# Fifteen load buffers, later modulation pieces, and block heads by halves of their banks, in a hybrid diffusion layer on one core

## The chip, the cores and the metric

The kernel runs on one core of one Trainium2 chip. The metric is device time in microseconds (us) of one execution. A profiled execution of the same program gives the span and the records of each engine: TensorE (PE, with its weight loads PEld), VectorE (DVE), ScalarE (ACT), GpSimd (POOL) and SyncE (SP), which issues most of the loads.

## The reference

One layer of a hybrid backbone is applied to 128 context tokens and 128 latent tokens, with shared weights. All arithmetic is float32.

```python
def block(x, mod, p, lb, s0_hg, s0_gdn, rows):
    shift1, scale1, gate1, shift2, scale2, gate2 = jnp.split(mod, 6, axis=-1)
    h = rmsnorm(x, p['norm1_g']) * (1.0 + scale1) + shift1
    (hq, hi, hgo, hff, hfb, cu, cv, gqkv, ggo, ga, gbeta, gates) = jnp.split(
        h @ p['w_in'], np.cumsum(IN_SIZES)[:-1].tolist(), axis=-1)
    o_a, s_hg = hgrn2_branch(hq, hi, hgo, hff, hfb, lb, p['hg_onorm_g'], s0_hg)
    o_b = chunk_mlp_branch(cu, cv, p['cm_vnorm_g'], p['cm_ws'], p['cm_bs'])
    o_c, s_gdn = gdn_branch(gqkv, ggo, ga, gbeta, ...)
    g_a, g_b, g_c = jnp.split(jax.nn.sigmoid(gates), 3, axis=-1)
    merged = (g_a * (o_a @ p['w_br_hg']) + g_b * (o_b @ p['w_br_cm']) + g_c * (o_c @ p['w_br_gdn']))
    x = x + gate1 * (merged @ p['w_out'])
    h2 = rmsnorm(x, p['norm2_g']) * (1.0 + scale2) + shift2
    x = x + gate2 * (jnp.square(jax.nn.relu(h2 @ p['w_ff1'])) @ p['w_ff2'])
    return x, s_hg, s_gdn
```

`mod` is `silu(c) @ w_mod + b_mod`, once with the context vector and once with the latent one. The model width is 2048, the hidden width of the channel sub-layer 8192. A final RMSNorm follows, and the final states of two branches are returned.

## The kernel before

All weights stream once through the chip, in units of 128 x 1024 floats (512 KB), and the 256 tokens stand still. A weight unit is loaded into a raw buffer by SP, then split into a rounded high part (`wh`, a cast on ACT) and a low part (`wl`, a subtraction on DVE); each product is three matmuls, high by high, low by high and high by low. The pair of split parts has its own buffers: three pairs, and two more during the opening (slots 8 and 9).

The program is written out by a planner in Python. `Clock` and `Meter` keep a planned time for each engine and buffer. `run_stream` walks through a list of steps. `issue()` emits loads as long as a raw buffer is in the list `raws`; `front()` emits the split of units ahead of their use, as long as a pair is in the list `pairs`; then the matmuls of the step are emitted. Between matmul groups `pump()` emits pieces of other work ("fillers": generators that run until they must wait), as long as ACT and DVE are planned less than a margin (1.8 us, 3.0 in the opening) ahead of TensorE. What is emitted later stands later in its engine's queue. Modulation pieces are the background filler and come last.

The opening (`start_steps`) has 88 units: 64 modulation units (`wmods`, for shift1 and scale1), which are used whole and unsplit, eight for each eighth of the width, and between them 16 units of the FF columns of `w_in` and 8 of the first half of FB. `lend` is 88. The raw buffers are three of their own (pool `rawp`, tag `raw`, used in turn) and, in the opening, five slots (3 to 7) of the large buffers, of which a load takes half. A slot goes back to the list only while fewer than `lend - 8` loads are issued; from then on the three own buffers are all there is. Modulation units give their buffer back when they are multiplied, the others when they are split.

The rest of the modulation (chunks 2 to 5) is 128 pieces done on DVE (`mods`): each is a load `mraw` of 512 KB and two multiply-and-sum passes (`junk<-mraw,cb`). The first two are loaded when the generator is created, at the 49th modulation unit; piece m is begun only when `quota(m)` units have been multiplied. `marks` are unit counts: a = 88, b before the last branch, and c, d, e about the end of the first sub-layer.

A block is one product with 1024 columns: 16 units (8 for the branch projections) into four PSUM banks of 512, out of six (`psb`), so that two banks of the next block are free while the last one is evacuated. In orientation B a bank takes two groups of 256 tokens, in A one group of 512 columns. A unit is one k-tile and runs through all four banks in order; `evac` empties them at the end, on ACT or DVE. For a branch (`branch`) evacuation is a multiplication of each bank by its gate on DVE, with `tail` as a filler behind it for the second and third branch. Most operations are recorded on line 173, that of the planner's wrapper, so tiles tell them apart: `raw` are loads, `pb` the block banks, `pf` the fillers' banks, `z` the large slots.

Of the kernel before, what the change touches and what calls it, by code (L numbers as in the profile page):

```python
# [7 lines left out]
F32 = mybir.dt.float32  # L8
F32R = mybir.dt.float32r
U8 = mybir.dt.uint8  # L10
AF = mybir.ActivationFunctionType
ALU = mybir.AluOpType
# [184 lines left out]
class Backbone:  # L197
# [194 lines left out]
    def run_stream(self, steps):  # L392


        nc = self.nc
        units = [s["unit"] for s in steps if "unit" in s]
        raw, hl = [], {}
        st = dict(dma=0, front=0)
        t = self.t

        raws = [None] * 3 + [3, 4, 5, 6, 7]
        pairs = [None] * 3 + [8, 9]

        def issue():
            while raws and st["dma"] < len(units):
                n = st["dma"]
                z = raws.pop(0)
                u = units[n]
                if z is None:
                    w = self.rawp.tile([P, NB], F32, tag="raw", name=self.nm("raw"))[:, :u.shape[1]]  # L410
                else:
                    w = self.slot(z, [P, NB])
                nc.sync.dma_start(w, u)
                raw.append((w, self.clock.dma + DMA1, z))
                st["dma"] += 1

        def front():
            n = st["front"]
            s = steps[n]
            st["front"] += 1  # L420
            if "unit" not in s:
                return
            w, at, z = raw.pop(0)
            if "whole" in s:
                hl[n] = (w, None, z, at)
                return
            c = w.shape[1]
            p = None if "own" in s else pairs.pop(0)
            if "own" in s:
                hi, lo = s["own"]()  # L430
            elif p is None:
                hi = self.hlp.tile([P, NB], F32R, tag="wh", name=self.nm("wh"))[:, :c]
                lo = self.hlp.tile([P, NB], F32R, tag="wl", name=self.nm("wl"))[:, :c]
            else:
                both = self.slot(p, [P, 2, NB], F32R)
                hi, lo = both[:, 0, :], both[:, 1, :]
            self.split(hi, lo, w)
            hl[n] = (hi, lo, p, max(t["act"], t["dve"]) + READY)
            if z is None or st["dma"] < self.lend - 8:
                raws.append(z)  # L440
            issue()

        issue()
        for i, s in enumerate(steps):
            while st["front"] < len(steps) and (pairs or not {"whole", "own"}.isdisjoint(steps[st["front"]])) and not ("hold" in s and st["front"] > i):
                if st["front"] > i and (raw and raw[0][1] > t["pe"] + 1.5 or len(hl) > 4) or not raw and "unit" in steps[st["front"]]:
                    break
                front()
            if s["kind"] == "mm":
                hi, lo, p, _ = hl.pop(i)  # L450
                s["do"](hi, lo)
                self.units += 1
                if "whole" in s:
                    if p is None or st["dma"] < self.lend - 8:
                        raws.append(p)
                    issue()
                    self.pump()
                    continue
                self.next = min((v[3] for v in hl.values()), default=0.0)
                self.pump()  # L460
                self.next = 0.0
                if "own" not in s and (p is None or st["dma"] < self.lend):
                    pairs.append(p)
            elif s["kind"] == "call":
                s["do"]()

    def block(self, units, nk, xh, xl, evac, orient="B", pre=None, late=False):


        nc = self.nc  # L470
        st = {}
        steps = []
        per = nk // len(units)
        cols = NB // per
        nb = max(4 // per, 1)

        def do(u, hi, lo):
            if u == 0:
                if pre is not None:
                    pre()  # L480
                st["b"] = [self.psb.tile([P, 512], F32, tag="b", name=self.nm("pb")) for _ in range(nb)]
            if u >= len(units) - 2:
                self.evac = self.t["pe"] + 24 * 0.12 * (len(units) - u)
            for k in range(u * per, u * per + per):
                off = (k - u * per) * cols
                ah, al = xh(k), xl(k)
                for c in range(8 if late else 0):
                    o = st["b"][c // 2][:, (c % 2) * 256:(c % 2) * 256 + 256]
                    for m, w in enumerate((hi, lo)):
                        nc.tensor.matmul(o, lhsT=w[:, c * P:c * P + P], rhs=ah, start=(k == 0 and m == 0 and c % 2 == 0),  # L490
                                         stop=False, skip_group_check=True)
                for c in range(2 * cols // min(cols, 512) if orient == "A" else 2 * nb):
                    if orient == "B":
                        o = st["b"][c // 2][:, (c % 2) * 256:(c % 2) * 256 + 256]
                        w = slice(off + c * P, off + c * P + P)
                        ops = ((hi[:, w], ah), (lo[:, w], ah), (hi[:, w], al))
                        first, lastc = c % 2 == 0, c % 2 == 1
                    else:
                        n = min(cols, 512)
                        z, v = divmod(c * n, cols)  # L500
                        o = st["b"][c * n // 512][:, c * n % 512:c * n % 512 + n]
                        w = slice(off + v, off + v + n)
                        t = slice(z * P, z * P + P)
                        ops = ((ah[:, t], hi[:, w]), (ah[:, t], lo[:, w]), (al[:, t], hi[:, w]))
                        first, lastc = c * n % 512 == 0, (c + 1) * n % 512 == 0
                    for j, (a, b) in enumerate(ops):
                        if late and j < 2:
                            continue
                        nc.tensor.matmul(o, lhsT=a, rhs=b, start=(k == 0 and j == 0 and first),
                                         stop=(k == nk - 1 and j == 2 and lastc), skip_group_check=True)  # L510
                    if lastc:
                        self.pump()
            if u == len(units) - 1:
                self.evac = np.inf
                evac(st["b"])

        for u in range(len(units)):
            steps.append(dict(kind="mm", unit=units[u], do=lambda hi, lo, u=u: do(u, hi, lo)))
        return steps


# [225 lines left out]
    def quota(self, m):  # L747

        a, b, c, d, e = self.marks
        if m < 20:  # L750
            return a - 12
        if m < 84:
            return a + (b - a) * (m - 20) / 64
        if m < 96:
            return b + (c - b) * (m - 84) / 12
        return d + (e - d) * (m - 96) / 32

    def mods(self, chs):
# [657 lines left out]
    def run(self):  # L1416
# [35 lines left out]
        def call(f):  # L1452
# [1 line left out]


        half = lambda i: [I["winh"][i, k] for k in range(8)]
        steps = self.start_steps(win(1, evac=act_evac("FF", 1, AF.Sigmoid)),
                                 self.block(half(0), 16, hh, hl, act_evac("FB", 2, AF.Sigmoid)))
        A = win(3, evac=act_evac("qA", 3, AF.Silu))
        B = self.block(half(1), 16, hh, hl, act_evac("FB", 2, AF.Sigmoid, 2))  # L1460
# [37 lines left out]
        def branch(i, half, oh, ol, order, pre=None):  # L1498
            def evac(b):
                g = getattr(self, f"gate{i}{half}")  # L1500
                if order == 0:
                    if half == 0:
                        self.merged = [None, None]
                    self.merged[half] = self.slot(1 + half, [P, 8, 256])
                if order == 2 and half == 0:
                    self.newH()
                for j in range(4):
                    m = flat(self.merged[half] if order == 0 else g, j)
                    nc.vector.tensor_tensor(out=m, in0=b[j], in1=flat(g, j), op=ALU.mult)
                if order > 0:  # L1510
                    self.before[i, half] = self.brgen[i, half] = self.add(tail(g), first=True)

            def tail(g):
                for j in range(4):
                    m = flat(self.merged[half], j)
                    nc.vector.tensor_tensor(out=m, in0=m, in1=flat(g, j), op=ALU.add)
                if order < 2:
                    return
                yield from self.together(*(turn(j) for j in range(4)))
# [461 lines left out]
```

## Time and profile before

| | us |
|---|---|
| median of 3 runs | 2014.07 |
| lowest, highest | 2012.14, 2018.22 |
| the profiled execution | 2009.21 |
| its span | 2007.1 |

| engine | busy us | share |
|---|---|---|
| PE | 1946.4 | 97% |
| DVE | 1409.7 | 70% |
| ACT | 952.1 | 47% |

Busy time of PE is modelled for pipelined matmuls, so it counts a slow matmul as busy too; the granted clock tells whether TensorE ran at full speed (its mean is 0.987 over the span). In the profile a row of the timeline has the start, the duration, the engine, the operation with its tiles, and in brackets how long the engine had been idle before it and what ended that. In a view of waits a row has the total, the number and the longest.

### The profile page before, as it was taken

How to read it: one execution, taken by the hardware profiler on the slowest of the kernel's cores; microseconds unless marked ns; L12 is line 12 of the kernel's file. 1: busy time of each engine (PE TensorE's matmuls, PEld its weight loads, DVE VectorE, ACT ScalarE, POOL GpSimd, SP SyncE). 2: the span in 40 equal slices, each digit the busy share in tenths (PEclk: the TensorE clock that was granted, in tenths of full speed). 3: DMA queues.
4: the chain of work that ended last, by engine and by line, in shares of the span. 5: the costliest groups of instructions: out<-in, count | busy, mean ns of one | idle time of the engine just before them, and what ended most of it. 6: DMA issues, size and time to landing. Idle time of an engine off the chain costs nothing.

```text
span 2007.1 us, 30574 instructions
## 1 busy us (share of the span) xinstructions
PE 1946.4 (97%) x11927; PEld 1711.1 (85%) x11927; DVE 1409.7 (70%) x2064; ACT 952.1 (47%) x1418; POOL 48.9 (2%) x120
## 2 busy tenths in 40 slices
PE   6989999999999999998999999899999999999997
PEld 3659988999888789887887888899988998998886
DVE  2348798978887998546775786767676676555466
ACT  3334645466645544466343444544444443344334
POOL 0000000000000001100000000000000000000000
PEclk9999999999989999998999999999999999999999
DMA  9987667666556767545768777566667676566664
GB/s 362 346 333 264 235 207 247 217 200 193 189 174 240 253 209 240 190 159 177 251 233 303 261 261 232 189 212 228 223 231 251 212 233 231 187 209 207 209 233 148
DMA packets 125216, 460.51 MB, mean 229 GB/s; under 512 B 14416, under 2 KB 14992, under 8 KB 122896
## 3 DMA queue, kind: packets, MB, share of 16 engines
q1 hardware_dynamic: 117072, 423.96, 62.1%
q0 software_dynamic: 7568, 34.35, 5.0%
q8 instruction: 93, 1.52, 0.3%
q14 instruction: 51, 0.42, 0.1%
q10 hardware_dynamic: 432, 0.26, 0.0%
HBM read 447.97 MB, written 10.53 MB: 228 GB/s over the span
## 4 chain that ended last, share of the span: by engine, by line
PE 81%; DVE 8%; DMA 5%; ACT 3%; issue 2%; SPq 0%; ACTq 0%; DVEq 0%
PE pb L173 73%; PE pf L173 8%; DVE wl L173 3%; DVE z L173 2%; DMA raw<-in_win 2%; DVE m L173 2%; ACT wh L173 1%; DVE junk L173 1%; DMA z<-in_win 1%; ACT z L173 1%; DMA z<-in_xT 0%; DMA raw<-in_wff2a 0%; DMA raw<-in_wff2c 0%; DMA raw<-in_winh 0%; DMA z<-in_winh 0%
## 5 line engine op out<-in xcount | busy, mean ns | idle before, releaser
L173 DVE TENSOR_TENSOR wl<-raw,wh 128x1024 fp32r<-128x1024 f32 x589 | 716.8, 1220 | 462.2 <-ACT wh L173 460.6
L173 ACT CAST wh<-raw 128x1024 fp32r<-128x1024 f32 x589 | 616.7, 1049 | 823.1 <-PE pb L173 696.9
L173 PE MATMUL pb<-Hh,wh 128*128 128x256 f32 x1864 | 530.6, 287 | 6.2 <-ACT wh L173 2.7
L173 PE MATMUL pb<-Hh,wl 128*128 128x256 f32 x1864 | 525.9, 285 | 2.5 <-DVE wl L173 2.5
L173 PE MATMUL pb<-Hl,wh 128*128 128x256 f32 x1864 | 512.2, 284 | 2.8 <-DVE Hl L173 2.8
L173 PE MATMUL pb<-wh,z 128*128 128x512 f32 x1368 | 430.0, 394 | 3.9 <-ACT z L173 3.9
L173 PEld LDWEIGHTS pb<-Hh,wh 128*128 128x128 f32 x1864 | 359.0, 193 | 17.4 <-issue 6.7
L173 PEld LDWEIGHTS pb<-Hh,wl 128*128 128x128 f32 x1864 | 359.2, 193 | 3.4 <-DVE wl L173 3.1
L173 PEld LDWEIGHTS pb<-Hl,wh 128*128 128x128 f32 x1864 | 350.5, 192 | 3.3 <-DVE Hl L173 3.2
L173 PE MATMUL pb<-wh,Hh 128*128 128x512 f32 (+1 forms) x800 | 315.8, 395 | 1.7 <-DVE z L173 1.4
L173 DVE SCALAR_TENSOR_TENSOR junk<-mraw,cb 128x1024 bf16<-128x1024 f32 x256 | 312.1, 1219 | 4.5 <-DMA mraw<-in_wmodr 3.3
L173 PEld LDWEIGHTS pb<-wh,z 128*128 128x128 f32 x1368 | 258.4, 189 | 61.0 <-ACT z L173 4.8
L173 PE MATMUL pb<-wl,Hh 128*128 128x512 f32 (+1 forms) x800 | 306.0, 383 | 1.1 <-DVE wl L173 1.1
L173 PE MATMUL pb<-wh,Hl 128*128 128x512 f32 (+1 forms) x800 | 305.9, 382 | 0.0
L173 PE MATMUL pb<-wl,z 128*128 128x512 f32 x684 | 269.4, 394 | 1.3 <-DVE wl L173 1.1
L173 PEld LDWEIGHTS pb<-wh,Hh 128*128 128x128 f32 x800 | 151.3, 189 | 30.4 <-DVE z L173 2.8
L173 PEld LDWEIGHTS pb<-wh,Hl 128*128 128x128 f32 x800 | 150.9, 189 | 29.6
L173 PEld LDWEIGHTS pb<-wl,Hh 128*128 128x128 f32 x800 | 151.4, 189 | 27.5 <-DVE wl L173 2.0
L173 PEld LDWEIGHTS pb<-wl,z 128*128 128x128 f32 x684 | 128.9, 188 | 31.1 <-DVE wl L173 2.9
L173 DVE TENSOR_TENSOR z<-z,z 128x512 f32<-128x512 f32 (+4 forms) x100 | 70.3, 739 | 16.2 <-ACT z L173 15.4
L173 DVE SCALAR_TENSOR_TENSOR cy<-z,par,cy 128x258 f32<-128x258 f32 (+1 forms) x192 | 53.6, 331 | 1.9
L173 PEld LDWEIGHTS pf<-m,z 128*128 128x128 f32 x384 | 48.9, 191 | 3.3 <-ACT z L173 0.7
(189 smaller groups left out, 1288.9 us busy)
## 6 DMA issues: line engine op xcount, KB each, us to landing
raw<-in_win SPq DMA_DIRECT2D x249, 512.0 KB, 4.1
raw<-in_wff SPq DMA_DIRECT2D x224, 512.0 KB, 4.1
mraw<-in_wmodr SPq DMA_DIRECT2D x128, 512.0 KB, 5.1
raw<-in_wbr SPq DMA_DIRECT2D x48, 512.0 KB, 4.1
z<-in_wmods SPq DMA_DIRECT2D x38, 512.0 KB, 6.7
raw<-in_wmods SPq DMA_DIRECT2D x26, 512.0 KB, 6.6
cb<-csd POOLq DMA_DIRECT2D x8, 1024.0 KB, 7.2
raw<-in_wouta SPq DMA_DIRECT2D x16, 512.0 KB, 4.3
```

Of the source, the lines that this page charges most:

```text
L173: return f(*a, **k)
```

## The change

- `run_stream` has 15 raw buffers in the opening: the three of `rawp`, each with a tag of its own, so that the one that was freed is the one that is taken, and both halves of six slots (3 to 7 and 0). The lent halves go back to the list only while fewer than `lend - 15` = 73 loads are issued.
- `quota`: pieces 0 to 23 are let go evenly over units 88 to 118, pieces 24 to 83 from there to b. Before, pieces 0 to 19 could start at unit 76.
- `block`: in blocks of four banks (36 of them; not FF, whose call has `skew=False`, and not the first block of the channel sub-layer, which is `late`) the first two k-tiles go through the first two banks and then through the other two. The pair of the first k-tile is held until the second is done (`hold_pair`, `kept`).
- `branch`: two of the four gate multiplications are emitted at the end of the block, two as a filler (`tail`), for the first branch too.

```diff
-        raws = [None] * 3 + [3, 4, 5, 6, 7]
+        lent = [self.slot(z, [P, 2, NB]) for z in (3, 4, 5, 6, 7, 0)]
+        raws = [0, 1, 2] + [t[:, h, :] for t in lent for h in range(2)]
+        last = self.lend - len(raws)
         pairs = [None] * 3 + [8, 9]
+        kept = []
...
-                if z is None:
-                    w = self.rawp.tile([P, NB], F32, tag="raw", name=self.nm("raw"))[:, :u.shape[1]]
+                if type(z) is int:
+                    w = self.rawp.tile([P, NB], F32, tag=f"raw{z}", name=self.nm("raw"), bufs=1)[:, :u.shape[1]]
                 else:
-                    w = self.slot(z, [P, NB])
+                    w = z
...
-            if z is None or st["dma"] < self.lend - 8:
+            if type(z) is int or st["dma"] < last:
                 raws.append(z)
...
-                if "own" not in s and (p is None or st["dma"] < self.lend):
-                    pairs.append(p)
+                if s.get("hold_pair"):
+                    kept.append(p)
+                elif "own" not in s:
+                    for p in kept + [p]:
+                        if p is None or st["dma"] < self.lend:
+                            pairs.append(p)
+                    kept.clear()
...
+            if skew and u == 0:
+                st["held"] = (hi, lo)
+                return part(0, hi, lo, 0)
+            if skew and u == 1:
+                part(1, hi, lo, 0)
+                part(0, *st["held"], 1)
+                return part(1, hi, lo, 1)
+            part(u, hi, lo)
...
-        if m < 20:
-            return a - 12
-        if m < 84:
-            return a + (b - a) * (m - 20) / 64
-        if m < 96:
-            return b + (c - b) * (m - 84) / 12
+        for n, lo, hi, n1 in ((0, a, a+30, 24), (24, a+30, b, 84), (84, b, c, 96)):
+            if m < n1:
+                return lo + (hi - lo) * (m - n) / (n1 - n)
...
-                for j in range(4):
-                    m = flat(self.merged[half] if order == 0 else g, j)
-                    nc.vector.tensor_tensor(out=m, in0=b[j], in1=flat(g, j), op=ALU.mult)
-                if order > 0:
-                    self.before[i, half] = self.brgen[i, half] = self.add(tail(g), first=True)
-
-            def tail(g):
+                for j in range(2):
+                    gated(j, b, g)
+                self.before[i, half] = self.brgen[i, half] = self.add(tail(b, g), first=True)
...
+            def tail(b, g):
+                for j in range(2, 4):
+                    yield 0.0
+                    gated(j, b, g)
+                if order == 0:
+                    return
+                yield 0.0
```

More of the change, by code (lines that the diff above doesn't have):

```diff
@@ L453, in run_stream @@
                 if "whole" in s:
-                    if p is None or st["dma"] < self.lend - 8:
+                    if type(p) is int or st["dma"] < last:
                         raws.append(p)
@@ L461, in run_stream, with block @@
                 self.next = 0.0
-                if "own" not in s and (p is None or st["dma"] < self.lend):
-                    pairs.append(p)
+                if s.get("hold_pair"):
[5 more added lines that the diff above has]
+                    kept.clear()
             elif s["kind"] == "call":
                 s["do"]()
-    def block(self, units, nk, xh, xl, evac, orient="B", pre=None, late=False):
+    def block(self, units, nk, xh, xl, evac, orient="B", pre=None, late=False, skew=True):
         nc = self.nc
@@ L475, in block @@
         nb = max(4 // per, 1)
+        skew = skew and nb == 4 and not late
         def do(u, hi, lo):
@@ L481, in do, with part @@
                 st["b"] = [self.psb.tile([P, 512], F32, tag="b", name=self.nm("pb")) for _ in range(nb)]
+            if skew and u == 0:
[6 more added lines that the diff above has]
+            part(u, hi, lo)
+        def part(u, hi, lo, half=None):
             if u >= len(units) - 2:
@@ L492, in do @@
                 for c in range(2 * cols // min(cols, 512) if orient == "A" else 2 * nb):
+                    if half is not None and c * 2 // (nb if orient == "A" else 2 * nb) != half:
+                        continue
                     if orient == "B":
@@ L517, in block @@
         for u in range(len(units)):
-            steps.append(dict(kind="mm", unit=units[u], do=lambda hi, lo, u=u: do(u, hi, lo)))
+            steps.append(dict(kind="mm", unit=units[u], do=lambda hi, lo, u=u: do(u, hi, lo), hold_pair=skew and u == 0))
         return steps
@@ L1456, in run @@
         half = lambda i: [I["winh"][i, k] for k in range(8)]
-        steps = self.start_steps(win(1, evac=act_evac("FF", 1, AF.Sigmoid)),
+        steps = self.start_steps(win(1, evac=act_evac("FF", 1, AF.Sigmoid), skew=False),
                                  self.block(half(0), 16, hh, hl, act_evac("FB", 2, AF.Sigmoid)))
@@ L1506, in evac, with gated @@
                     self.newH()
-                for j in range(4):
-                    m = flat(self.merged[half] if order == 0 else g, j)
-                    nc.vector.tensor_tensor(out=m, in0=b[j], in1=flat(g, j), op=ALU.mult)
-                if order > 0:
-                    self.before[i, half] = self.brgen[i, half] = self.add(tail(g), first=True)
-            def tail(g):
+                for j in range(2):
+                    gated(j, b, g)
+                self.before[i, half] = self.brgen[i, half] = self.add(tail(b, g), first=True)
+            def gated(j, b, g):
+                m = flat(self.merged[half] if order == 0 else g, j)
+                nc.vector.tensor_tensor(out=m, in0=b[j], in1=flat(g, j), op=ALU.mult)
+            def tail(b, g):
[5 more added lines that the diff above has]
+                yield 0.0
                 for j in range(4):
```

## The prediction

> **What bounds the kernel now.** I read the page first, then busy time by stages, the chain of waits and TensorE's timeline through the opening, then SP's, and TensorE's waits after it.
>
> ```profile
> span 2007.1 us, 30574 instructions
> PE 1946.4 (97%) x11927; PEld 1711.1 (85%) x11927; DVE 1409.7 (70%) x2064; ACT 952.1 (47%) x1418; POOL 48.9 (2%) x120
> PE 81%; DVE 8%; DMA 5%; ACT 3%; issue 2%; SPq 0%; ACTq 0%; DVEq 0%
> ```
>
> TensorE sets the end; 19% of the chain lies elsewhere. Busy time by stages (length; then PE, PEld, DVE, ACT and POOL; granted clock, DMA share, GB/s) shows where:
>
> ```profile
> 0.00:50.00 50.00, 32.84 (x183) 17.91 (x186) 13.91 (x27) 18.06 (x30) 1.95 (x7) 0.97 0.96 362
> 50.00:100.00 50.00, 49.55 (x351) 33.22 (x345) 15.67 (x22) 17.80 (x27) 0.00 (x0) 1.00 0.93 347
> 125.00:150.00 25.00, 19.52 (x115) 14.11 (x115) 13.17 (x20) 5.70 (x9) 0.00 (x0) 0.84 0.74 287
> 150.00:172.30 22.30, 19.13 (x127) 18.63 (x126) 18.60 (x29) 13.03 (x19) 0.00 (x0) 0.80 0.80 267
> 172.30:218.40 46.10, 46.10 (x387) 46.10 (x386) 39.13 (x51) 18.13 (x19) 0.53 (x1) 1.00 0.81 273
> 250.00:300.00 50.00, 50.00 (x266) 43.00 (x265) 49.43 (x75) 22.37 (x28) 0.73 (x1) 1.00 0.62 205
> ```
>
> The opening (64 modulation loads, 16 loads of FF, 8 of FB) runs to 172.30; from there TensorE has no gap in 172 to 218 at clock 1.00. The opening's second half is the bad place: the granted clock is 0.84 and 0.80 and the DMA engines fall to 0.74.
>
> ```profile
> 109.99 0.28 PE L173 MATMUL pf<-ident,cs 128*32 128x128 f32 x1 [1.25 <-DVE modc L173]
> 123.38 0.39 PE L173 MATMUL pb<-Hh,wh 128*128 128x256 f32 x1 [1.41 <-ACT wh L173]
> 124.64 0.57 PE L173 MATMUL pb<-Hh,wl 128*128 128x256 f32 x1 [0.87 <-DVE wl L173]
> 131.54 0.62 PE L173 MATMUL pf<-raw,cst 128*32 128x512 f32 x2
> 148.14 0.39 PE L173 MATMUL pb<-Hh,z 128*128 128x256 f32 x1 [3.87 <-ACT z L173]
> 163.80 0.39 PE L173 MATMUL pb<-Hl,wh 128*128 128x256 f32 x1 [2.76 <-DVE Hl L173]
> 172.30 0.28 PE L173 MATMUL pb<-Hh,wh 128*128 128x256 f32 x1
> 112.68 9.58 DMA z<-in_win
> 124.64 2.71 PE pb L173 x11
> 230.06 0.89 PE pf L173 x8
> 230.95 2.87 PE pb L173 x24
> 137.52 1.85 PE pf L173 x12
> ```
>
> The brackets are waits. The load of 112.68 took 9.58 us and TensorE waited for it at 123.38. After the wait 11 matmuls took 2.71, 0.246 each; 24 take 2.87 later, 0.120 each. So a wait costs itself and some us at half clock.
>
> ```profile
> 125.95 0.42 SPq L173 DMA_DIRECT2D raw<-in_win  x1
> 132.63 7.11 SPq L173 DMA_DIRECT2D raw<-in_wmods  x2
> 139.79 0.90 SPq L173 DMA_DIRECT2D mraw<-in_wmodr  x2
> 140.80 0.37 SPq L173 DMA_DIRECT2D raw<-in_win  x1
> 149.37 0.33 SPq L173 DMA_DIRECT2D raw<-in_win  x1
> raw<-in_win SPq DMA_DIRECT2D x249, 512.0 KB, 4.1
> GB/s 111 416 298 419 413 411 408 412 413 275 403 376 276 372 307 368 366 399 336 371 371 387 251 358 370 369 322 416 417 408 301 127 89 402 415 240 272 276 310 208
> ```
>
> These are SP's issues and the rate in 40 slices of 0 to 172. The last eight loads have only three buffers, so SP issues one at 125.95, two in 132.63 to 139.74, and then two modulation pieces ahead of the next weight: 127 and 89 GB/s.
>
> **The change part by part.**
>
> *Fifteen buffers.* A matrix is 512 KB; slices of 408 to 419 GB/s move one in 1.27 us. TensorE eats 3 modulation pieces in 1.85 and a weight in 2.87: a round of 8 pieces, 3 weights and the small matmuls (0.89) costs it 14.4, the 11 loads 14.0, and TensorE idles for 17 of the first 50 us. With buffers to run ahead, loads stay in front. So waits on loads up to the piece at 131.54 go: 1.25 at 109.99, 1.41 at 123.38, and in 123.38 to 131.54 (8.16) all but 2.87 + 0.89 = 3.76, so 4.40. I add 1.0 for the small starts. Sum 8.1. The two first modulation pieces now follow the load of m58, not m55, which helps the same wait; the engine that issues them is SP, past three more loads, and nobody reads them before load 88.
>
> What is late next is the tail. The 12 lent halves are no longer handed back once 73 of the 88 loads are issued (before: five, at 80), so loads 76 to 87 share three buffers, where 82 to 87 did. Bookkeeping of the list: 73 to 75 take the three own buffers, 76 (a weight) waits until 73 is read, and so on in four rounds. One link is landing 4.1, cast and subtraction:
>
> ```profile
> L173 DVE TENSOR_TENSOR wl<-raw,wh 128x1024 fp32r<-128x1024 f32 x589 | 716.8, 1220 | 462.2 <-ACT wh L173 460.6
> L173 ACT CAST wh<-raw 128x1024 fp32r<-128x1024 f32 x589 | 616.7, 1049 | 823.1 <-PE pb L173 696.9
> L173 DVE SCALAR_TENSOR_TENSOR junk<-mraw,cb 128x1024 bf16<-128x1024 f32 x256 | 312.1, 1219 | 4.5 <-DMA mraw<-in_wmodr 3.3
> ```
>
> From the reading of load 73 as zero: weight 76 is issued at 0.6, landed 4.7, cast 5.8, so TensorE, done with its three pieces at 1.9, waits to 5.9 and ends the weight at 9.3. Its buffer frees at 7.1; the next pieces end at 12.6; weight 80 is issued when the first of them is read, 9.9 to 11.9, and starts at 15.2 to 17.2; the last pieces end at 21 to 24, weights 83 to 87 follow at 22 to 24, 26 to 30, 31 to 37, and the stage ends at 40 to 47. The ends are two orders of handing back (weights are split up to four steps ahead, so who frees first is open). Before it took 172.30 - 131.54 = 40.8. I take 43.3, near the middle: +2.5, kept from -1 to +6. Waits of 3 to 4 us stand in it twice, as before, so half clock stays for some of it. In the Trainium skill, "TensorE: Matmul & The Clock Gate", Part 1, the clock halves after an idle window of about 3.4 us; here a wait of 1.41 with the 0.87 behind it was enough, so the measurement decides.
>
> Opening: -8.1 + 2.5 = -5.6.
>
> *Is DMA the limit instead?* The row of slices has 408 to 419 wherever buffers were free. The Trainium skill, "DMA: Bandwidth & Descriptors", Where 436 GB/s comes from, puts HBM at about 358 GB/s a core. By that the 83 loads to the last modulation piece (43.5 MB) with an estimated 5 MB of others would end at an estimated 138, and buffers would gain nearly nothing; by the slices they end at 120. The trace does not agree with the page, and I follow the trace.
>
> *Modulation pieces.* Up to 20 could start at load 76, now 24 spread over loads 88 to 118. Fifteen half pieces lie in 136 to 172, each 1.22 on VectorE; they come behind 172 now, 18 us of work. Cover: VectorE is free for 7.0 of 46.1 there, and only for 0.6 of 50 in 250 to 300. Pieces are last in the filler order, and TensorE waits for none of them before the norm of the second sub-layer, so I cost it 0 (from -1 to +4: if the cover is gone, one late piece in each of a few full stretches).
>
> *Halves of banks.* Thirty-six blocks of four banks change. Gain: the first two k-tiles use two banks for 2.87 in place of 1.44, so the other banks are needed later. Waits for banks at a head, and all longer waits of this kind:
>
> ```profile
> PE pb L173 <- DVE z L173: 4.0, 2, 2.6
> PE pb L173 <- DVE wl L173: 2.2, 4, 0.8
> 663.02 0.50 PE L173 MATMUL pb<-wh,Hh 128*128 128x512 f32 x1 [1.44 <-DVE z L173]
> 740.13 0.39 PE L173 MATMUL pb<-Hh,wh 128*128 128x256 f32 x1 [2.56 <-DVE z L173]
> ```
>
> Two heads in 36 wait. Each can save 1.4: -2.8. Cost: the first pair of split weights is held until the second k-tile is done. Its last reader ends 1.44 later, and the split of the fourth k-tile enters the queues of ACT and VectorE one k-tile (2.87) later, behind more fillers, while its need stays; the second k-tile is needed 1.44 sooner.
>
> ```profile
> ACT wh L173 <- PE pb L173: 696.9, 418, 7.2
> 418.12 0.28 PE L173 MATMUL pb<-Hh,wh 128*128 128x256 f32 x1
> 424.40 1.23 DVE L173 TENSOR_TENSOR wl<-raw,wh 128x1024 fp32r<-128x1024 f32 x1 [2.06 <-ACT wh L173]
> 1592.91 0.28 PE L173 MATMUL pb<-Hh,wh 128*128 128x256 f32 x1
> 1599.55 2.35 DVE L173 TENSOR_TENSOR wl<-raw,wh 128x1024 fp32r<-128x1024 f32 x2
> ```
>
> In 418 of 589 splits ACT waits for the pair, so it is free and has only the 1.44 to absorb: split 1.05 + 1.22 with hops is 2.4, release to need is 4.3, 1.9 spare. In a block with full ACT, the one from 418.12, the fourth split ends at 425.63 and is needed at 418.12 + 3 x 2.87 + 0.12 = 426.85: 1.2 spare, which 2.87 later in the queue turns into a wait of up to 1.6. By the same count the block from 1592.91 has its fourth subtraction ended near 1600.76 (the first of the two) and needs it at 1601.67, 0.9 spare. I count eight blocks so tight, these the first and the last. At 0.45 on average +3.5; bounds 0 (all absorbed) and 36 x 0.7 = 25.
>
> *Branch evacuation in two parts.* The same four multiplications; the last two banks aren't wanted by the next block (six banks), so 0. If VectorE is late, the block after waits, up to 1.3 at six places.
>
> Sum: -5.6 + 0 - 2.8 + 3.5 = -4.9 on the profiled execution. Its span is 2007.1 and its time 2009.21; the median of the runs shown is 2014.07, so I forecast 2014.07 - 4.9, about 2009.
>
> **Rivals.**
>
> *More comes off the opening.* The tail's work is 8 x 0.62 + 7 x 2.87 and 2 us of small matmuls, 27; were only the two 4 us waits left at full clock it would be 35, not 43.3: -13.2, and 2001. With heads unharmed 1998. For it: fifteen half pieces and their loads leave the tail, where the wait at 163.80 stands behind them. Against: three buffers.
>
> *The loads are full already.* Shares are 0.96 and 0.93 in the first 100 us. If 362 and 347 GB/s are all that eight DMAs and more give together, TensorE waits at 123 as before but for two pieces (2.5), and the tail's 2.5 takes it back: 2014. Against it are the slices of 408 to 419. The Trainium skill's limit, cited above from "DMA: Bandwidth & Descriptors", says the same as this rival.
>
> *The tail eats it.* It is 47 long and half clock costs some us more: +8, and 2015.
>
> *Slower: late splits at every head.* One mechanism: the held pair puts the fourth split behind fillers in most blocks. At 0.55 each over 36 blocks 20 us: -8.4 + 20, and 2025. It decides from 0.4 each (14.4 - 8.4 = +6). For it: VectorE is busy 49.43 of 50 in 250 to 300. Against: ACT waits for the release in 418 of 589.
>
> **How the numbers follow.** About 0.3%, 6 us here, is what a measurement can tell from no change. Chances: forecast 0.40 (own range 2004 to 2013), more off the opening 0.20, loads full 0.11, tail 0.12, late splits 0.17. Faster than 2008: 0.20 and half the forecast's, 0.40. Slower than 2020: 0.17. Same: 0.43. The range runs from 1998 to 2021, and leaves out about 0.1 on each side: the better half of nothing but the best tails, and most of the late splits.
>
> **What would show it.** Opening: the piece after 123 starts near 123 in place of 131.54, DMA above 400 GB/s until about 105, then starved; the stage ends near 166.7 in place of 172.30. Tail: two waits of 3 to 4 us at weights 76 and 80 behind loads, with clock 0.5 after. Pieces: none read before the stage's end, VectorE fuller behind it. Heads: waits at 663 and 740 shorter by 1.4, new ones for wl at the fourth k-tile of about eight blocks. Wrong if the loads never exceed 365 GB/s on average while buffers are free, if the tail is below 37 or above 48, or if fourth k-tiles wait in more than 20 blocks.

## The result and the profile after

The changed kernel takes 2001.14 us (median; 1999.77 to 2003.34) against 2013.11 (2010.22 to 2018.22) for the kernel before, a ratio of 0.9949 [0.9935, 0.9963]: 12 us less. The forecast was 4.9 less, 2009, in a range of 1998 to 2021. The profiled execution spans 1998.9 instead of 2007.1 us. First the lines of the page that answer to those of before, and busy time by stages of the changed kernel (length; PE, PEld, DVE, ACT, POOL; clock, DMA share, GB/s):

```profile
span 1998.9 us, 30561 instructions
PE 1941.3 (97%) x11927; PEld 1707.3 (85%) x11927; DVE 1407.2 (70%) x2064; ACT 952.6 (48%) x1419; POOL 49.0 (2%) x120
PE 89%; DMA 4%; DVE 3%; ACT 2%; issue 1%; POOL 0%; ACTq 0%; POOLq 0%; DVEq 0%
```

```profile
0.00:50.00 50.00, 30.98 (x161) 15.72 (x162) 13.35 (x27) 18.06 (x30) 1.95 (x7) 0.96 0.98 374
50.00:100.00 50.00, 50.00 (x356) 35.71 (x356) 15.67 (x22) 18.14 (x28) 0.00 (x0) 0.98 1.02 403
125.00:150.00 25.00, 15.77 (x90) 11.87 (x91) 4.08 (x6) 4.86 (x8) 0.00 (x0) 0.82 0.45 157
150.00:174.65 24.65, 21.61 (x153) 19.61 (x153) 9.93 (x11) 12.22 (x17) 0.00 (x0) 0.90 0.57 184
```

PE's work is the same 11927 matmuls; its share of the chain grows from 81% to 89%. The loads do run ahead (403 GB/s from 50 to 100 us, 347 before), and then starve: 157 GB/s from 125 to 150, where it was 287. In the first 50 us nothing is won (TensorE is busy for 30.98, before for 32.84). TensorE's and SP's rows show the opening's second half:

```profile
128.77 1.92 PE L173 MATMUL pf<-raw,cst 128*32 128x512 f32 x12
134.59 0.58 PE L173 MATMUL pb<-Hh,wh 128*128 128x256 f32 x1 [3.91 <-ACT wh L173]
146.75 0.39 PE L173 MATMUL pb<-Hh,z 128*128 128x256 f32 x1 [3.76 <-ACT z L173]
160.46 0.38 PE L173 MATMUL pb<-Hh,wh 128*128 128x256 f32 x1 [2.17 <-ACT wh L173]
174.65 0.39 PE L173 MATMUL pb<-Hh,z 128*128 128x256 f32 x2
```

```profile
113.36 0.90 SPq L173 DMA_DIRECT2D mraw<-in_wmodr  x2
129.86 0.33 SPq L173 DMA_DIRECT2D raw<-in_winh  x1
130.70 5.45 SPq L173 DMA_DIRECT2D raw<-in_wmods  x3
```

SP issues nothing from 114.3 to 129.86, because only three buffers are left; weight 76 is late by 3.91, weight 80 by 3.76, a third by 2.17. The opening ends at 174.65: 2.35 later than before (172.30), not 5.6 earlier. One opening can differ from the next of the same kind by more than that (last section), but the mean of the three profiled ones with these buffers is 175.7, and of the five with the old ones 172.1.

So the gain lies behind the opening. I split each profiled execution at the first matmul of three blocks: qA (the opening's end), uB (the first input block of the gmlp branch), and br10 (the gmlp's first branch block, which needs its finished output).

| | opening | qA to uB | uB to br10 | br10 to end | span |
|---|---|---|---|---|---|
| before | 172.3 | 563.7 | 210.3 | 1060.8 | 2007.1 |
| after | 174.65 | 561.1 | 200.9 | 1062.3 | 1998.9 |

Of the 8.2 us, +2.35 is the opening, -2.6 is qA to uB, -9.4 is uB to br10, +1.4 the rest. Part of the 9.4 is only moved: this stretch has 1336 matmuls before and 1312 after, and the other 24 come behind br10. TensorE's waits in it add up to 10.2 us before and 4.2 after. What happened between uB and br10 is in TensorE's timeline, in which pf<-tp,z are the gmlp's four products, pf<-ident,z beside them the transposes of the GDN's last part (its norm and gate), and pf<-m,z the GDN's products. Before:

```profile
922.42 1.95 PE L173 MATMUL pf<-tp,z 128*128 128x128 f32 x16
937.75 0.63 PE L173 MATMUL pf<-ident,z 128*128 128x128 f32 x4 [1.15 <-DVE z L173]
939.46 2.89 PE L173 MATMUL pf<-tp,z 128*128 128x128 f32 x16 [1.09 <-DVE z L173]
946.26 0.80 PE L173 MATMUL pb<-wh,z 128*128 128x512 f32 x1 [3.90 <-ACT z L173]
```

After:

```profile
897.13 1.05 PE L173 MATMUL pf<-tp,z 128*128 128x128 f32 x8
899.39 1.05 PE L173 MATMUL pf<-tp,z 128*128 128x128 f32 x8
903.02 1.05 PE L173 MATMUL pf<-tp,z 128*128 128x128 f32 x8
906.65 1.05 PE L173 MATMUL pf<-tp,z 128*128 128x128 f32 x8
940.13 1.05 PE L173 MATMUL pf<-m,z 128*128 128x128 f32 x8
```

Before, the GDN finishes first: two of the gmlp's four products stand behind block g10's last weight and behind the GDN's last part, and br10 waits for them (1.15, 1.09 and 3.90, then matmuls at half clock to 950.9). After, all four are through by 907.7, and the GDN is still at work when br10 begins at 936.62. Its last state goes out 37 us later than before (POOL's rows, before and after), which costs nothing, since br20, the block that needs it, begins 170 us later:

```profile
905.05 0.69 POOL L173 DMA_DIRECT2D out_stgd<-tp  x1 [21.89 <-ACT tp L173]
```

```profile
942.10 0.69 POOL L173 DMA_DIRECT2D out_stgd<-tp  x1 [15.65 <-ACT tp L173]
```

### The profile page after: what moved, and what is told of

It reads as the page before. It is cut to its first block, busy times and chain, and to the rows that moved or that the text cites. A ratio compares the mean times of both kernels' runs of the same rounds, so it can differ in the third digit from the quotient of the medians.

```text
span 1998.9 us, 30561 instructions
## 1 busy us (share of the span) xinstructions
PE 1941.3 (97%) x11927; PEld 1707.3 (85%) x11927; DVE 1407.2 (70%) x2064; ACT 952.6 (48%) x1419; POOL 49.0 (2%) x120
## 4 chain that ended last, share of the span: by engine, by line
PE 89%; DMA 4%; DVE 3%; ACT 2%; issue 1%; POOL 0%; ACTq 0%; POOLq 0%; DVEq 0%
PE pb L173 80%; PE pf L173 9%; DVE wl L173 1%; DMA raw<-in_win 1%; DVE z L173 1%; ACT wh L173 1%; DMA raw<-in_wff2c 1%; DMA par<-in_par 1%; DMA z<-in_win 1%; DVE m L173 0%; ACT tp L173 0%; DMA z<-in_wmods 0%; ACT z L173 0%; DMA z<-sp 0%; DMA z<-in_s0gd 0%
## 5 line engine op out<-in xcount | busy, mean ns | idle before, releaser
L173 PE MATMUL pb<-Hh,wh 128*128 128x256 f32 (+1 forms) x1856 | 529.1, 288 | 9.3 <-ACT wh L173 8.4
L173 PE MATMUL pb<-Hh,wl 128*128 128x256 f32 (+1 forms) x1856 | 525.5, 286 | 4.3 <-DVE wl L173 4.3
L173 PE MATMUL pb<-Hl,wh 128*128 128x256 f32 (+1 forms) x1856 | 510.7, 285 | 0.0
L173 PEld LDWEIGHTS pb<-Hh,wh 128*128 128x128 f32 (+1 forms) x1856 | 358.8, 193 | 20.5 <-ACT wh L173 11.3
L173 PEld LDWEIGHTS pb<-Hh,wl 128*128 128x128 f32 (+1 forms) x1856 | 359.0, 193 | 6.3 <-DVE wl L173 6.0
L173 PEld LDWEIGHTS pb<-Hl,wh 128*128 128x128 f32 (+1 forms) x1856 | 350.0, 193 | 0.1
```

The costliest lines, as they stand in the source:

```text
L173: return f(*a, **k)
```

## The experiments

After this comparison I held that the buffers lose time at the opening's tail, and that one part alone makes the gain behind it: the due times (theory Q) or the halves with the gate products (theory H). The rival, O, was that any edit moves the planner and the wait ahead of 946 goes by luck. The theory that the gain is the order of two fillers, gmlp ahead of the GDN's end, was tested from the second round on.

**Each part alone.** The kernel before with one part of the change.

```
quota_only:   only quota() of the change
buffers_only: only the buffer list of the change
heads_branch: only the halves of banks and the two later gate products
```

> The kernel before with the new due times of the modulation pieces, nothing else. Theory Q (the later and evenly spread due times give the 13 us that the change won between 517 and 946 us): the wait of TensorE at 936 to 946 us (6.5 us and 10 us at half clock) goes, the opening stays at 172.3, the time is 2001 to 2004, ratio 0.994 to 0.996. Theory H (the halves of banks with the split gate products give it): the time is that of before within 3 us, and the wait before 946 stays. Theory O (any change of the order moves the planner, and the wait at 936 goes by luck): anything between 2000 and 2016, the wait present or not without a pattern.

> The kernel before with the 15 load buffers and their order alone. Theory of the tail (the three buffers left for the last 12 loads cost what the earlier loads won): the opening's end moves by +1 to +4 us, from 172.3 to 174 to 176, with waits of about 4 us at weights 76 and 80, and the time stays within 4 us of before. My prediction's step (opening earlier by 5.6): end at 166.7, time 2008. Theory O: the opening as in the first, the time anywhere from 2000 to 2016.

> The kernel before with the halves of the banks and the two later gate products alone; buffers and due times as before. Theory H: 2000 to 2004 (the 13 us are won from 517 to 946 us, the opening stays at 172.3, so 2 us better than the whole change at best: 1999). Theory Q: the heads at 663 and 740 us lose their waits of 1.4 and 2.6 us, some fourth k-tiles wait 0.2 to 0.9, the time is 2009 to 2015, and the wait at 936 to 946 stays.

Measured: 2011.0 (0.999 [0.998, 1.0]), 2011.9 (0.9992 [0.9981, 1.0003]) and 2016.04 (1.0016 [1.0003, 1.0029]). No part alone makes the gain: by the medians they add up to about +2, by the ratios to about 0, where all together give -12. So neither of my two single-part theories held. The wait before br10 is there in all three; with the halves alone:

```profile
946.44 2.05 PE L173 MATMUL pf<-tp,z 128*128 128x128 f32 x16 [1.08 <-DVE z L173]
953.02 0.80 PE L173 MATMUL pb<-wh,z 128*128 128x512 f32 x1 [4.52 <-ACT z L173]
```

**Two parts at a time.** The changed kernel with the old buffers, and with the old due times.

```
quota_and_heads:   raws = [None] * 3 + [3, 4, 5, 6, 7]   # as before
buffers_and_heads: quota() as before
```

> The changed kernel with the buffers of before: new due times, halves of banks and the two later gate products. Theory of the order (these together, and neither alone, put the gmlp ahead of the GDN's last groups): 1995 to 2000, with no wait before br10, and the opening ending at 171 to 172.5, so 2 to 4 below the change. Theory that each part has a worth of its own (they were measured at -1.2 and +3.3 us): 2012 to 2016.

> The changed kernel with the due times of before: 15 buffers, halves of banks and the two later gate products. Theory of the order (in program order two of the gmlp's four products stand behind block g10 here): the wait of 4 to 5 us before br10 is there again, and the time is 2012 to 2019, 11 to 18 above the change. Rival (the change's gain comes from buffers and halves together): 2000 to 2004.

Measured: 1995.88 (0.9915 [0.9897, 0.9932]) and 2011.01 (0.9989 [0.998, 0.9997]). Due times and halves together are the whole gain, and without the fifteen buffers it is 5 us larger. With the old due times the wait is back, as the order theory said, though the time is 1 us below its range. Two gmlp products are behind the block again:

```profile
940.40 2.05 PE L173 MATMUL pf<-tp,z 128*128 128x128 f32 x16 [1.08 <-DVE z L173]
946.97 0.80 PE L173 MATMUL pb<-wh,z 128*128 128x512 f32 x1 [4.52 <-ACT z L173]
```

**The order by itself.** The kernel before, with none of the change, and one wait in the GDN's generator ahead of its last part.

```
+        while self.before.get("B") not in self.dead:   # "B" is the gmlp
+            yield W
         self.och, self.ocl = ...
         yield from self.norm_gate(self.otC, ...)
```

> The kernel before with one wait more in the GDN filler: its last part (the norm and gate of the whole result) starts only when the gmlp filler is done, so that the gmlp's four products are issued ahead of block br10 in program order. Theory of the order (what the change won between 735 and 946 us is that the gmlp comes ahead of the last of the GDN, so that nothing is left of it when br10 must begin): the waits of 1.20, 1.14 and 4.11 us before 946 and the half clock behind them go, 6 to 9 us less, 2003 to 2006, with none of the change's three edits. Rival (the wait only moves: the GDN's last part is then late for br20, which needs it): the wait at 946 goes, another of 3 to 8 us comes before br20 at 1125, and the time is 2010 to 2014. Rival (the change's gain is in TensorE's many small waits, by the halves of banks, not in this wait): 2009 to 2013.

Measured: 2006.49 (0.997 [0.9958, 0.9981]), 6.1 us less, at the near edge of what the order theory gave (6 to 9 less; its 2003 to 2006 is missed by half a us). The four products are issued ahead of br10, and the waits around them are small:

```profile
928.60 1.13 PE L173 MATMUL pf<-tp,z 128*128 128x128 f32 x8 [1.41 <-DMA tp<-in_wsT]
933.01 1.05 PE L173 MATMUL pf<-tp,z 128*128 128x128 f32 x8
946.32 0.50 PE L173 MATMUL pb<-wh,z 128*128 128x512 f32 x1 [1.37 <-ACT z L173]
```

From uB to br10 it takes 202.3 instead of 210.3, and no new wait came up before br20 (br10 to the end takes 1060.9, before 1060.8). The order alone gives 8 of the 9.4 us (here 16 matmuls come behind br10 instead of 24); two lines do that without either edit.

**The lent buffers kept.** The changed kernel with one number changed; then the same with the eight buffers of before instead of fifteen.

```
after_last88:  -        last = self.lend - len(raws)
               +        last = self.lend
eight_kept:    quota_and_heads, with self.lend instead of self.lend - 8 (twice)
```

> The changed kernel with one number changed: the lent buffers go back into the list until the last of the 88 loads is issued, not until the 76th. Theory of the tail: SP has no gap from 113.8 to 129.9 us, the waits at weights 76, 80 and 87 (4.05, 3.90 and 2.33 with 1.14 each) and their half clock go, and the opening ends at 160 to 165 instead of 174.65: the time is 1987 to 1993, 8 to 14 below the change. Rival (the opening's second half is set by VectorE's and ScalarE's casts and by the loads' rate, not by the buffers): the end moves by under 3 us, the time is 1998 to 2002. Rival (the lent buffers are wanted by the work right behind the opening, so they come free later and FB or the first fillers wait): the opening ends at 160 to 165, but the blocks up to 420 us give it back, and the time is 1998 to 2005.

> The changed kernel with the eight buffers of before, whose five lent ones go back into the list until load 88 is issued, not until the 80th. Theory of the tail (what the opening loses is the lent buffers' early going, whatever their number): the opening ends at 160 to 164 and the time is 1985 to 1990, as with fifteen kept (1987.5), so the fifteen are worth nothing. Rival, my prediction's step (more loads in flight take 8 us of waits off the opening's first 131 us): with eight it ends at 165 to 170, the time is 1991 to 1996.

Measured: 1987.54 (0.9875 [0.9857, 0.9893]) and 1991.06 (0.99 [0.9882, 0.9918]). With fifteen kept, the stage from 125 to 150 us has 24.12 of 25 busy at full clock, and the waits at weights 76 and 80 are gone; qA starts at 161.6, and from there on all is as in the changed kernel (1824.1 and 1824.2 us):

```profile
125.00:150.00 25.00, 24.12 (x175) 17.91 (x171) 8.58 (x13) 12.06 (x19) 0.00 (x0) 1.00 0.67 268
```

With eight kept qA starts at 166.8, and the wait at a weight's load that the kernel before has at 123 is still there (this load, issued at 115.59, took 9.64):

```profile
126.35 0.58 PE L173 MATMUL pb<-Hh,wh 128*128 128x256 f32 x1 [2.68 <-ACT wh L173]
127.61 0.58 PE L173 MATMUL pb<-Hh,wl 128*128 128x256 f32 x1 [0.68 <-DVE wl L173]
125.00:150.00 25.00, 22.11 (x124) 15.74 (x124) 8.21 (x10) 9.04 (x13) 0.00 (x0) 0.80 0.83 319
```

The first kernel is as the tail theory had it, and both its rivals fall: casts and rate don't set the second half, and the work behind the opening gives nothing back. The second is not: it came out, at the border of the two ranges, as my prediction's step would have it. Keeping the buffers is worth 5 us with eight (opening 172.1 to 166.8 in the profiled executions, time 1995.88 to 1991.06). What seven more buffers are worth is less sure: 8 us by the profiled openings (158.9 is the mean of the five with fifteen kept), but 1 to 7 by the medians of the three that differ in little else (1983.85 to 1989.6, against 1991.06); for 1987.54 the intervals overlap.

**What holds on that base.** Fifteen kept, and: no halves; no halves but the GDN's added wait; gate products as before; due times 40 units behind the mark.

```
last88_no_halves:            skew = False
last88_no_halves_gmlp_first: the same, and the wait of gmlp_first
last88_no_later_products:    all four gate products in evac, as before
last88_due40:                a+30 -> a+40
```

> The kernel with the lent buffers kept until load 88 (1987.5 us), with its blocks' first two k-tiles whole again; the two later gate products stay. Theory of the order (two of the gmlp's products stand behind g10 again): the wait before br10 is there, 1994 to 2001, although the fourth k-tiles wait less. Rival (the halves' own worth counts): without them 1 to 4 us less by the fourth k-tiles, or up to 4 more by the heads at 663 and 740 us, and no wait before br10: 1984 to 1992.

> Fifteen buffers kept until load 88, no halves of banks (1996.7 us), and the GDN's last part put behind the gmlp by one wait. Theory of the order (the halves' whole worth is that they put the gmlp ahead): the wait before br10 goes, uB to br10 takes 201 to 205 us instead of 216, the time is 1983 to 1989. Rival (the halves have a worth of their own beside it, in the heads or in the fillers' pace): 1990 to 1995.

> Fifteen buffers kept until load 88 (1987.5 us), with a branch block's four gate products all at its end as before. My prediction's step (the two later products are worth nothing): 1985 to 1990, the gmlp's order as it was. Rival (VectorE's 1.4 us at the end of each branch block hold up the next block's wl): 1990 to 1996, with longer waits at the blocks behind br00, br01 and br10.

> Fifteen buffers kept until load 88 (1987.5 us), with the first 24 modulation pieces due over 40 units behind the mark instead of 30. Theory that the order holds over a range of due times: 1984 to 1991, no wait before br10, uB to br10 in 200 to 204 us. Rival (the gmlp's order is an accident of this one setting): the wait before br10 is back, 1995 to 2003.

Measured: 1996.74 (0.9919 [0.9903, 0.9934]), 1991.14 (0.9905 [0.9886, 0.9924]), 1983.85 (0.9865 [0.9842, 0.9887]) and 1989.6 (0.9884 [0.9865, 0.9903]). Without the halves the order is lost and br10 waits again:

```profile
927.88 2.05 PE L173 MATMUL pf<-tp,z 128*128 128x128 f32 x16 [1.08 <-DVE z L173]
934.46 0.79 PE L173 MATMUL pb<-wh,z 128*128 128x512 f32 x1 [4.53 <-ACT z L173]
```

The added wait brings uB to br10 from 216.0 down to 204.6, as expected, but 2.5 of it come back behind br10 (1065.7 instead of 1063.2), and the time, 1991, is 2 us above the order theory's range and in the rival's: the halves keep a small worth beside the order, or the later GDN a small cost; these runs don't part them. The two later gate products are worth nothing that shows (the part behind the opening is 1825.5 without and 1824.1 with them). Ten more units of delay leave the order, and 1824.4 behind the opening, so the order does not hang on this one setting.

All profiled executions, sorted by what the gmlp's order is (the median is that of all executions; the profiled one of "due 40" is its fastest, 1983.85):

| | opening | uB to br10 | all behind the opening | median |
|---|---|---|---|---|
| **two gmlp products behind g10** | | | | |
| before | 172.3 | 210.3 | 1834.8 | 2011 to 2014 |
| due times alone | 170.5 | 214.9 | 1838.4 | 2011.0 |
| fifteen buffers alone | 175.2 | 211.1 | 1836.8 | 2011.9 |
| halves and gate products alone | 171.1 | 218.3 | 1843.6 | 2016.0 |
| buffers and halves | 177.3 | 208.2 | 1831.2 | 2011.0 |
| fifteen kept, no halves | 157.2 | 216.0 | 1840.5 | 1996.7 |
| **gmlp ahead by one added wait** | | | | |
| before + wait | 176.2 | 202.3 | 1828.1 | 2006.5 |
| fifteen kept, no halves + wait | 160.3 | 204.6 | 1829.1 | 1991.1 |
| **gmlp ahead by due times and halves** | | | | |
| after | 174.65 | 200.9 | 1824.2 | 2001.1 |
| old buffers | 170.2 | 201.1 | 1823.6 | 1995.9 |
| eight kept | 166.8 | 201.4 | 1824.2 | 1991.1 |
| fifteen kept | 161.6 | 201.8 | 1824.1 | 1987.5 |
| fifteen kept, old gate products | 157.4 | 201.5 | 1825.5 | 1983.9 |
| fifteen kept, due 40 | 157.7 | 201.8 | 1824.4 | 1989.6 |

The opening goes with the buffers. The rest goes in the main with the order: 1823.6 to 1829.1 with the gmlp ahead, 1831.2 to 1843.6 without. The 12 us of spread among the six without are not explained by the order. The best versions keep the fifteen buffers to the last load, with due times and halves: 1984 to 1990, 11 to 17 below the change.

## Why the prediction was right or wrong

The kernel is faster, by 12 us where 4.9 were forecast, but for a reason that the prediction doesn't hold. That the time lies inside the range, and the sign is right, is luck: the opening, the largest gain of the sum (-5.6), lost 2.35, and what was won comes from a step that the sum has at 0. Step by step:

- *Opening waits gone, -8.1.* To the piece ahead of weight 76 it came to -2.8 (131.54 to 128.77). The loads ran ahead as I said. What the step left out is that a landed load is not a cast weight. TensorE's and ScalarE's rows of the changed kernel, then ScalarE's of the kernel before:

```profile
47.85 0.38 PE L173 MATMUL pb<-Hh,wh 128*128 128x256 f32 x1 [1.02 <-ACT wh L173]
49.11 0.58 PE L173 MATMUL pb<-Hh,wl 128*128 128x256 f32 x1 [0.88 <-DVE wl L173]
49.49 0.41 PE L173 MATMUL pb<-Hl,wh 128*128 128x256 f32 x1
49.71 0.41 PE L173 MATMUL pb<-Hh,wh 128*128 128x256 f32 x1
113.88 0.38 PE L173 MATMUL pb<-Hh,z 128*128 128x256 f32 x1 [0.92 <-ACT z L173]
115.14 0.39 PE L173 MATMUL pb<-Hh,z 128*128 128x256 f32 x1 [0.88 <-DVE z L173]
115.36 0.28 PE L173 MATMUL pb<-Hl,z 128*128 128x256 f32 x1
115.49 0.40 PE L173 MATMUL pb<-Hh,z 128*128 128x256 f32 x2
```

```profile
44.56 1.65 ACT L173 ACTIVATE tp<-tp,modc,gs 128x128 f32<-128x128 f32 x4 [2.90 <-DVE tp L173]
46.24 0.62 ACT L173 CAST Hh<-tp 128x512 fp32r<-128x512 f32 x1
46.77 1.04 ACT L173 CAST wh<-z 128x1024 fp32r<-128x1024 f32 x1
```

```profile
41.58 1.04 ACT L173 CAST wh<-z 128x1024 fp32r<-128x1024 f32 x1
44.79 1.65 ACT L173 ACTIVATE tp<-tp,modc,gs 128x128 f32<-128x128 f32 x4 [2.17 <-DVE tp L173]
```

  Before, the cast of the third weight stands ahead of the modulation of the input chunk (41.58 and 44.79) and TensorE doesn't wait for it. In all eight kernels with fifteen buffers it stands behind (46.77 and 44.56), so TensorE waits 1.02 + 0.88 at 47.85 although the weight has landed. The same happens at the fifteenth weight, 0.92 + 0.88 at 113.88. From its first matmul to that of the next, the third weight takes 7.49 instead of 4.91 and the fifteenth 6.04 instead of 4.89. With the 1.02 ahead of the third that is 4.8 of the 5.3 us that are missing. Why the planner emits these casts later was not traced. I had named what is late next as the tail alone.
- *Tail, +2.5.* It measured 45.9 (128.77 to 174.65) against 40.8: +5.1, the upper half of my 40 to 47. Place and mechanism were right (waits of 3.91 and 3.76 at weights 76 and 80; 3 to 4 was written), and there was a third of 2.17 at the next three-buffer round. The term was too small by 2.6.
- *Modulation pieces, 0.* This is the step that failed: the term is 0 in the sum, and with the halves it carries the whole gain, although due times alone changed the time by only 0.1%. I asked who waits for a piece. The question left out is who is held up by it: pieces take VectorE's time, and what the planner can place beside them sets how far the GDN is when the gmlp starts. VectorE from 740 to 865, before and after:

```profile
740.00:865.00 125.00, 123.40 (x917) 116.19 (x918) 83.84 (x139) 55.37 (x95) 14.34 (x42) 1.00 0.61 202
```

```profile
740.00:865.00 125.00, 121.28 (x857) 112.21 (x856) 103.61 (x175) 54.30 (x85) 12.39 (x36) 1.00 0.71 238
```

  VectorE has 20 us more work there and TensorE 60 matmuls less. That the fuller VectorE is what holds the GDN back is argued from these rows, not shown, and it is not enough by itself: in the 125 us from uB's first matmul VectorE is busy for 87.0 before and 106.0 after, but also for 98.4 with due times alone and 97.6 with fifteen kept and no halves, which both have the old order. Why it takes both edits stays open.
- *Halves, -2.8 and +3.5.* The two heads' waits went (1.44 to none at 657.02; 2.56 to 0.38 at 737.86), 3.6 us in all. The cost was nearly right in size and wrong in place: only two fourth k-tiles wait for wl (0.21 and 0.41, in blocks k and uB), not eight, but second and third k-tiles wait too (0.38 in uB, 0.23 and 0.57 in br01, 0.65 in g21), which I had named as needed sooner and not priced. The six add up to 2.45. No late block waits: from 1311.41 to 1899.56 the changed kernel takes 588.15 us, the same blocks 588.15 before, so the spare of 0.9 that I counted at 1601.67 was enough. The halves alone made the kernel 3 to 4 us slower. There four fourth k-tiles do wait (0.52, 1.40, 0.85 and 0.25), but from the opening to uB that is offset (563.6, before 563.7); the 8 us are lost from uB to br10 (218.3). There TensorE's waits add up to 15.2 us, before to 10.2; three of them are for the GDN's own loads (1.20, 2.26 and 2.35).
- *Gate products, 0.* As measured.
- *Rivals.* "Loads are full already" fell with 403 GB/s. "The tail eats it" is right for the opening, which lost 2.35, and wrong on the time. "More comes off the opening" named 2001 and is wrong in its mechanism (and its sum with the heads unharmed is 1997.4, not 1998). Its opening would end at about 158, and with the fifteen buffers kept it does: 157.2 to 161.6. "Late splits" stays at two blocks.
- *What would make it wrong:* tail and fourth k-tiles stayed inside their bounds. None of the signs looked at the wait ahead of 946, whose three pieces (1.15, 1.09 and 3.90) are the largest sum of waits at one place behind the opening in the profile of before. I left it out because no edit names the gmlp.

## What to carry to other kernels

In a kernel whose fillers a planner places by simulated engine times, moving work that nobody waits for still moves what is placed around it: look for the forced finishes in the profile (here 1.09 and 3.90 us ahead of br10) and ask of each edit whether it changes who is late there. If an order is worth time, write it down as a wait of its own: two lines gave 8 us between uB and br10, which otherwise came only with two unrelated edits together. More buffers help only for as long as they are in the list: follow the list to the last load.

## What the runs showed of the hardware

The same opening varied by 4 to 5 us between profiled executions (171.1, 172.3 and 176.2 with the old buffers and due times; 157.2 to 161.6 in the five with fifteen kept), while all behind it repeated within 2 us (1823.6 to 1825.5 over six kernels with that order). So between these executions the spread arises in the first 177 us. The clock, below, makes some of it; the rest was not traced.

Waits of the same length, at the same place, halve the clock in one execution and not in another. The pair of 1.02 + 0.88 at the third weight stands in all eight kernels with fifteen buffers, and the program up to there is the same. Behind it the matmuls come 0.21 to 0.22 apart, to about 52.4, in the changed kernel (rows 49.49 and 49.71 above), and so they do with fifteen kept; in the six others they come 0.12 apart. The pair of 0.92 + 0.88 at the fifteenth weight is the other way round in the changed kernel (0.12), and halves the clock in two others. With the fifteen buffers alone, at the third weight:

```profile
50.57 0.39 PE L173 MATMUL pb<-Hh,wl 128*128 128x256 f32 x1 [0.88 <-DVE wl L173]
50.80 0.28 PE L173 MATMUL pb<-Hl,wh 128*128 128x256 f32 x1
50.91 0.28 PE L173 MATMUL pb<-Hh,wh 128*128 128x256 f32 x1
```

With buffers and halves, at the fifteenth:

```profile
113.91 0.58 PE L173 MATMUL pb<-Hh,z 128*128 128x256 f32 x1 [0.88 <-DVE z L173]
114.29 0.41 PE L173 MATMUL pb<-Hl,z 128*128 128x256 f32 x1
114.50 0.63 PE L173 MATMUL pb<-Hh,z 128*128 128x256 f32 x2
```

The granted clock is 0.50 from 49.11 to 52.30 in the changed kernel, and 1.00 from 50.57 to 53.50 with the fifteen buffers alone. The halved clock costs 1.4 to 1.5 us here: from the third weight to the fourth it takes 7.5 instead of 6.05, from the fifteenth to the sixteenth 7.5 instead of 6.03. So neither the length of the waits nor the work that stands before them decides. The Trainium skill, "TensorE: Matmul & The Clock Gate", Part 1, has a free-running activity window, idle for about 3.4 us before the clock halves. That the phase of such a window decides fits these rows, but no run here shows it; that 3.4 us of idling are needed does not fit, since neither pair of waits reaches it.
